# Soft-routed mixture of experts on one Trainium2 core: two mixed stages become an unmixed P1 pair with a split and an unmixed P2 pair, and the preparation of later weights moves between stages

## The chip, the cores and the metric

The kernel runs on one core of one Trainium2 chip. The metric is the time of one execution in microseconds (us), as the device reports it; lower is better. Times are told as the median of several executions.

## What is computed

```python
probs = softmax(router_logits)                 # [16, 512, 8]
output = zeros((16, 512, 2048))
for e in range(8):
    output += probs[:, :, e:e+1] * matmul(x, expert_weights[e])   # [8192,512] x [512,2048]
```

That is one long matrix product: 8192 tokens by a contraction of 8 x 512 = 4096, in which the left operand is x times a token's probability for the expert, by 2048 columns.

## The kernel before

**Three levels of Strassen-Winograd.** The tokens are cut into 16 pairs q of two blocks of 256 (h = 2q and 2q+1), the experts into two halves of four, the columns into two halves of 1024. A pair needs seven products P1 to P7 in place of eight block products (`product(r, q)`, r from 1 to 7). Each product is 256 tokens by a contraction of 2048 by 1024 columns and is cut once more: `STEPS` = 1, 5, 6, 2, 7, 3, 4, seven steps of 8 matmuls each (128 tokens, 128 of the contraction, 512 columns; `Product.step`). Some steps accumulate on a bank that a Vector addition has just written (`Product.post`).

**Stages.** Two products make a stage (`add`), and TensorE runs their steps in turn: 14 slots of 8 matmuls. Stages 0 to 5 hold P1 of the pairs 2 to 13; stage 6 holds P2 of 13 and P1 of 14, stage 7 P2 of 14 and P1 of 15 (the mixed stages); stages 8 to 14 hold the other P2. From stage 15 on come P5, P6, P7, P4, P3.

**The split.** Where both products of a stage have the same right operand, `third(stage, r)` cuts their steps 1 and 5 a third time: the 4 x 8 matmuls of 512 columns become 14 parts of 4 matmuls of 256 columns (`Third.part`, run by `run_third`), with four more sums `s` of left operands, two partial copies per step on ScalarE and two additions `ps<-ps,d` per step on VectorE. Before the change the stages 0 to 5 are split for P1, 8 to 12 for P2, and six stages of P3. In a split stage the order on TensorE is: the parts x1, x5, q1, q5; slot 12 of the stage before, which was held back; x2, q2, x6, q6; slot 13 of the stage before, also held; x7, q7, x3, q3, x4, q4; then the slots from 4 on.

**Where operands come from.** VectorE multiplies x by probabilities into tiles `z` (`times`), and makes sums `s`, `s2` (tile `d`) and `i` (`z<-z,d`, `queue_i`). These are tasks of one queue, written out by a planner (`slack`, `need`, `later`) that keeps two clocks and fixes the order of VectorE's instructions when the program is built; on the chip each engine works strictly in its program's order. Additions of results (`h<-ps,h`) and `ps<-ps,d` are not in the queue: they stand in the program at their step.

**x blocks.** A block of x that is not yet kept transposed is read with a cast by GpSimd's queue (`XBlock.begin`, at the stage two ahead, slot 1) and turned by four transposing DMAs of SyncE's queue for two blocks (`XBlock.finish`, slot 7, line 463). The raw block goes into a buffer of `xpool` (9 buffers), or, for h in `X_ROOMS`, into half of a tile `u`, which two blocks share (`x_room`). There is one buffer of `u`.

**Wedges and casts.** A wedge (`wedge`, `wedge_at`) makes an eighth of the weights for P5, P6 and P7: it casts two blocks of expert weights into a tile `w` by GpSimd's queue, and some slots later (`then`) queues three tasks on VectorE: t3, which writes a tile `u` (the same single buffer), t1 and t2; each is followed by a store to DRAM (`wd<-u`, `wd<-w`) on GpSimd's queue. `cast21` casts the blocks of B21, the raw weights of P2, by the same queue; `sums_at` then queues their sums.

**Results.** P1's results go to DRAM (`kept<-h`), and P2 adds them: it fetches them again on SyncE's queue (`fetch_at`, `h<-kept`) or, where P1 of the same pair has just run, takes the tile (`base = products[1, q].o`).

**Queues.** SyncE (lines 123 and 463), GpSimd (line 126) and ScalarE issue DMAs in order: one that has to wait for its buffer holds everything behind it on that queue.

Of the kernel before, what the change touches and what calls it, by code (L numbers as in the profile page):

```python
# [31 lines left out]
def kernel(  # L32
# [78 lines left out]
    def tt(o, a, b, op):  # L111
        dve(nc.vector.tensor_tensor(out=o, in0=a, in1=b, op=op))  # L112
# [12 lines left out]
    def pool(o, i, **how):  # L125
        note(nc.gpsimd.dma_start(out=o, in_=i, **how))  # L126
# [15 lines left out]
    def new_z():  # L142
        return zpool.tile([P, K8, HQ], f16, name="z", tag="z")
# [248 lines left out]
    queue = deque()  # L392
    clock = {"pe": 0.0, "dve": 0.0}

    class Task:
# [5 lines left out]
        def run(self):  # L401
            self.done = True
            clock["dve"] += self.cost
            self.make()
# [5 lines left out]
    def need(task):  # L410
        if task is not None and not task.done:
            flush(task)
            clock["pe"] = max(clock["pe"], clock["dve"])

    def later(cost, make, first=False):
        t = Task(cost, make)
        (queue.appendleft if first else queue.append)(t)
        return t

    def slack(slot=SLOT):  # L420
        if clock["pe"] > 30.0:
            clock["dve"] = max(clock["dve"], clock["pe"])
        clock["pe"] += slot
        while queue and clock["dve"] < clock["pe"] - LAG:
            queue.popleft().run()
# [3 lines left out]


    x_dram = {}
    X_ROOMS = range(16, 28, 2)
    rooms = {}

    def x_room(h):

        if h % 4 == 0:
            two = new_u().rearrange("p (two k) t -> p two (k t)", two=2)
            for i in range(2):
                rooms[h + 2 * i] = two[:, i].rearrange("p (j m) -> p j m", j=HQ // P)  # L440
        return rooms.pop(h)

    class XBlock:
# [5 lines left out]
        def begin(self):  # L449
# [5 lines left out]
            elif self.t is None:  # L455
                self.xs = x_room(self.h) if self.h in X_ROOMS else xpool.tile([P, HQ // P, H], f16, name="xs", tag="x")
                pool(self.xs, x_f[ds(self.h * HQ, HQ), :].rearrange("(j p) h -> p j h", p=P))
# [34 lines left out]
    class Left:  # L492
# [48 lines left out]
                tt(self.s2, self.t[0][:, :, ds(HP, HP)], self.t[0][:, :, ds(0, HP)], SUB)  # L541
            self.task["s2"] = later(0.61, make)

        def queue_i(self):
            if self.into is not None:
                self.queue_make(1)

            def make():
                self.i = new_z()
                two = "p k (h t) -> p h k t"  # L550
                tt(self.i.rearrange(two, h=2), self.t[1].rearrange(two, h=2),
                   self.s2.unsqueeze(1).to_broadcast([P, 2, K8, HP]), SUB)
            self.task["i"] = later(1.14, make)

        def op(self, p):
            need(self.task[{1: 0, 5: 0, 6: "s2", 2: 1, 4: 1, 3: "i", 7: "i"}[p]])
# [168 lines left out]
    def out_rows(q, odd, cols, tn):  # L725
        t, n = tn
        return out_f[ds((2 * q + odd) * HQ + t * HP, HP), ds(cols * NH + n * NB, NB)]

    def to_out(q, odd, cols, **how):
        return lambda tn, o: pool(out_rows(q, odd, cols, tn), o, **how)  # L730
# [20 lines left out]
    def at(stage, slot, make):  # L751
        hooks.setdefault((stage, slot), []).append(make)

    def add(*products):
        stages.append(products)
        return len(stages) - 1
# [40 lines left out]
    def kept_rows(q):  # L797
        return lambda tn: kept[q][tn[1], ds(tn[0] * HP, HP), :]

    def product(r, q, **how):  # L800
        left, loads = left_of(r, q)
        lefts[r, q] = left
        p = None
        if r == 1:
            def sink(tn, o):
                pool(kept_rows(q)(tn), o)
            p = Product(right[1], left, sink)
        elif r == 2:
            if q >= 13:
                base = products[1, q].o.__getitem__  # L810
            else:
                base = bases[2, q] = Base(kept_rows(q))
            p = Product(right[2], left, to_out(q, 0, 0), base)
        elif r == 5:
            bases[6, q] = m1 = Base(kept_rows(q))
            m1.task = {}

            p = Product(right[5], left, to_out(q, 1, 0))
        elif r == 6:
            m1 = bases[6, q]  # L820

            def base(tn):
                need(m1.task[tn])
                return m1.t[tn]
            p = Product(right[6], left, to_out(q, 0, 1), base)
            if q in KEEP:
                left.kept = dram.tile([P, 2, K8, HQ], f16, name=f"kept_left_{q}")
        elif r == 7:
            if q < 14:
                base = bases[7, q] = Base(lambda tn: out_rows(q, 0, 1, tn))  # L830
            else:
                base = products[6, q].o.__getitem__
            p = Product(right[7], left, to_out(q, 1, 1), base)
        elif r == 4:
            p = Product(right[4], left, to_out(q, 1, 0, accum_op=ADD), products[7, q].o.__getitem__)
        else:
            p = Product(right[3], left, to_out(q, 0, 1, accum_op=ADD), **how)
        p.loads = loads
        products[r, q] = p
        return p  # L840

    products = {}
    forget = lambda *hs: [xs.pop(h, None) for h in hs]
# [30 lines left out]
    thirds, splits, held = {}, {}, []  # L874
# [20 lines left out]
    def before(stage, n):  # L895
        for make in hooks.get((stage, n), ()):
            make()

    def after(stage, n):
        if n == 1:  # L900
            queue_lefts(stage + 1)
        if n == late.get(stage, 1):
            start_loads(stage + 2)
        if n == 5:
            store_loads(stage + 1)
        if n == 7:
            finish_loads(stage + 2)

    def run_third(stage):
# [15 lines left out]
                product.post(p)  # L925
        after(stage, 4)

    def run(stage):
        some = stages[stage]
        for p in some:  # L930
            p.left.queue_i()
        slots = [(p, i) for i in range(len(some[0].steps)) for p in some]

        def one(n):
            p, i = slots[n]
            before(stage, n)
            p.step(p.steps[i])
            slack()
            p.post(p.steps[i])
            after(stage, n + 1)  # L940
        first = 0
        if stage in thirds:
            run_third(stage)
            first = 4
        end = len(slots) - (2 if stage + 1 in thirds else 0)
        for n in range(first, end):
            one(n)
        for n in range(end, len(slots)):
            held.append(lambda n=n: one(n))
# [3 lines left out]
            at(stage, slot, lambda tn=tn: base.fetch(tn))  # L953


    for q in range(2, 14, 2):
        add(product(1, q), product(1, q + 1))
    for q in range(13, 15):
        add(product(2, q), product(1, q + 1))
    forget(*range(0, 26, 2))  # L960
    rest = [15] + list(range(13))
    for i in range(0, 14, 2):
        k = add(product(2, rest[i]), product(2, rest[i + 1]))
        for slot, tn in zip((8, 10, 12, 13), INNER):
            for q in rest[i:i + 2]:
                if q < 13:
                    fetch_at(k if tn == (1, 0) else k - 1, 3 if tn == (1, 0) else slot, bases[2, q], tn)
    xs.clear()
    k5 = add(product(5, 0), product(5, 1))
# [3 lines left out]
    some = product(6, 15)  # L973
# [5 lines left out]
    some = product(4, order7[-1])  # L979
# [50 lines left out]
            send("t2", b)  # L1030
        return casts, [t3, t1, t2]

    def wedge_at(stage, slot, kn, e, then):
        made = []

        def begin():
            casts, made_ = wedge(kn, e)
            casts[0]()
            made.extend(made_ + casts[1:])

        def go_on():
            for make in made[:3]:
                later(1.14, make)
        at(stage, slot, begin)
        at(stage, slot + 4, lambda: made[3]())
        at(*then, go_on)

    b21, t1, t2, t3 = {}, {}, {}, {}

    def cast21(kn, e):  # L1050
        if e == 0:
            b21[kn] = new_w()
        cast_w(21, kn, e, b21[kn][:, ds(e * C, C), :])

    for i, kn in enumerate(((0, 0), (0, 1), (1, 1), (1, 0))):
        for e in range(2):
            at(*((i + 0,5), (i + 0,12))[e], lambda kn=kn, e=e: cast21(kn, e))

    def sums_at(stage, slot, r, of, ps):
        def go():  # L1060
            if right[r].w is None:
                right[r].sums = right[r].build(of)
            for p in ps:
                right[r].queue_sum(right[r].sums, p)
        at(stage, slot, go)
    sums_at(5, 4, 2, b21, (5,))
    sums_at(5, 6, 2, b21, (6,))
    sums_at(5, 8, 2, b21, (7,))
    sums_at(5, 12, 2, b21, (4,))
    for i, (kn, e) in enumerate((kn, e) for kn in ((0, 0), (1, 0), (1, 1)) for e in range(2)):  # L1070
        wedge_at(4 + i, 3, kn, e, {5:(10,6)}.get(i,(4+i,11)))

    def fetch_at_w(stage, slot, of, what, kn):
        at(stage, slot, lambda: of.__setitem__(kn, fetch_w(what, kn)))
# [4 lines left out]
    made = {}  # L1079
# [193 lines left out]
            post(p)  # L1273
    finish.step, finish.post = step_at_end, post_at_end

    for stage in (0,1,2,3,4,5):
        third(stage, 1)
    splits[1].t = early_t
    for stage in (8,9,10,11,12):
        third(stage, 2)  # L1280
    at(7,2, splits[2].queue)

    for q in KEEP:
        for k, slot in enumerate((1, 5)):
# [61 lines left out]
```

## Time and profile before

| | us |
|---|---|
| median of 3 runs (lowest to highest) | 1365.53 (1364.66 to 1365.61) |
| the profiled execution | 1364.02 |
| its span, from the first to the last instruction | 1362.1 |
| TensorE busy | 1355.7 (100%) |
| VectorE busy | 1149.8 (84%) |
| GpSimd busy (it issues DMAs) | 409.4 (30%) |
| ScalarE busy | 203.6 (15%) |

The profile names engines PE (TensorE's matmuls), PEld (its weight loads), DVE (VectorE), ACT (ScalarE), POOL (GpSimd) and SP (SyncE; SPq and POOLq are their queues). A row of the timeline gives the start and the length in us, the engine, the line, the operation with the tiles it writes and reads (out<-in), and how often it stands in a row; in brackets stands the idle time ahead of it and what ended it. A row of the waits gives who waited for whom: us in total, how often, the longest. In rows of the windows, the busy time of each engine in a stretch is followed by its count of instructions. Matmuls overlap, so the length of one is not the pace: the pace is read from starts.

### The profile page before, as it was taken

To read this page: it belongs to the slowest core of one execution; us is meant where nothing else is said; L and a number is where in the kernel's file an instruction comes from. 1 tells how busy PE (TensorE), PEld (TensorE's weight loads), DVE (VectorE), ACT (ScalarE), POOL (GpSimd) and SP (SyncE) were. 2 spreads that over 40 slices of the span, in tenths; PEclk is the share of its full clock that TensorE was granted. 3 is DMA by queue.
4 is the path that set the end of the run, shared out by engine and by line. 5 is a ranking of instruction groups with operands and counts; after the bars stand their busy time and mean duration, and the time that the engine had idled before them with its cause. 6 is when DMAs were issued, how large, how long until landed. Compare 5 with 4: busy or idle time off the path is not lost.

```text
span 1362.1 us, 18545 instructions
## 1 busy us (share of the span) xinstructions
PE 1355.7 (100%) x6801; PEld 662.8 (49%) x6801; DVE 1149.8 (84%) x1415; ACT 203.6 (15%) x386; POOL 409.4 (30%) x644
## 2 busy tenths in 40 slices
PE   9999999999999999999999999999999999999998
PEld 4555545565444444444444444444444444456554
DVE  7976789988999788787887888888889797998873
ACT  3332311111011111111111100000000000123221
POOL 3123233322223333324332122332333322232232
PEclk9999999999999999999999999999999999999999
DMA  9999999999999999999999977988898979999897
GB/s 192 229 249 247 232 232 310 286 309 356 314 307 273 315 339 286 294 280 281 328 275 334 351 241 206 221 246 204 230 243 234 241 204 296 291 223 247 198 206 117
DMA packets 195691, 356.43 MB, mean 262 GB/s; under 512 B 53136, under 2 KB 87184, under 8 KB 191248
## 3 DMA queue, kind: packets, MB, share of 16 engines
q0 software_dynamic: 88048, 183.02, 56.7%
q1 hardware_dynamic: 99488, 132.25, 32.3%
q10 hardware_dynamic: 8064, 39.99, 8.0%
q8 instruction: 53, 0.87, 0.3%
q14 instruction: 38, 0.31, 0.1%
HBM read 214.47 MB, written 167.97 MB: 281 GB/s over the span
## 4 chain that ended last, share of the span: by engine, by line
PE 98%; DMA 1%; issue 1%; POOL 0%; DVE 0%; ACT 0%; POOLq 0%
PE ps L132 98%; DMA w<-in_expert_weights_dram 1%; DMA out_dram<-h 0%; POOL w L126 0%; POOL kept L126 0%; POOL out_dram L126 0%; DVE h L112 0%; ACT h L638 0%; ACT h L1270 0%; DVE ps L112 0%; POOL ident L216 0%; POOLq L126 0%; POOLq L216 0%; POOLq L1330 0%
## 5 line engine op out<-in xcount | busy, mean ns | idle before, releaser
L132 PE MATMUL ps<-w,z 128*128 128x512 f16 x5144 | 1098.4, 373 | 0.4 <-DMA w<-in_expert_weights_dram 0.3
L132 PEld LDWEIGHTS <-z 128*128 128x128 f16 x5280 | 516.4, 98 | 578.1 <-DMA w<-in_expert_weights_dram 0.5
L126 POOL DMA_DIRECT2D out_dram<-h x380 | 249.4, 662 | 739.5 <-ACT h L638 366.1
L112 DVE TENSOR_TENSOR h<-ps,h 128x512 f32<-128x512 f32 x415 | 284.3, 687 | 157.5 <-PE ps L132 137.2
L112 DVE TENSOR_TENSOR z<-xT,pT 128x2048 f16<-128x2048 f16 x216 | 261.7, 1218 | 2.9 <-DMA xT<-w 2.9
L132 PE MATMUL ps<-w,d 128*128 128x512 f16 x880 | 199.1, 379 | 0.0
L132 PEld LDWEIGHTS <-d 128*128 128x128 f16 x880 | 86.1, 98 | 100.3
L112 DVE TENSOR_TENSOR z<-z,d 128x2048 f16<-128x2048 f16 x110 | 131.6, 1217 | 0.0
L638 ACT COPY h<-ps 128x512 f32<-128x512 f32 x64 | 37.6, 587 | 492.5 <-PE ps L132 486.8
L112 DVE TENSOR_TENSOR w<-w 128x1024 f16<-128x1024 f16 (+2 forms) x88 | 100.1, 1146 | 0.8
L627 ACT COPY h<-ps 128x512 f32<-128x512 f32 x90 | 52.8, 587 | 282.8 <-PE ps L132 267.2
L112 DVE TENSOR_TENSOR d<-z 128x1024 f16<-128x1024 f16 x110 | 74.4, 687 | 1.4
L624 ACT COPY h<-ps 128x512 f32<-128x512 f32 x90 | 51.7, 590 | 126.7 <-PE ps L132 119.8
L126 POOL DMA_DIRECT2D kept<-h x56 | 30.6, 547 | 106.7 <-ACT h L627 72.7
L132 PEld LDWEIGHTS <-s 128*128 128x128 f16 x544 | 53.2, 98 | 10.8 <-issue 1.3
L126 POOL DMA_DIRECT2D wd<-w x78 | 46.5, 621 | 38.4 <-DVE w L112 32.6
L132 PE MATMUL ps<-t,s 128*128 128x256 f16 x408 | 55.7, 273 | 0.8 <-DVE ps L112 0.8
L126 POOL DMA_DIRECT2D w<-in_expert_weights_dram x65 | 48.8, 771 | 11.9 <-issue 8.0
L112 DVE TENSOR_TENSOR ps<-ps,d 128x256 f32<-128x256 f32 x68 | 28.4, 430 | 24.9 <-PE ps L132 24.8
L112 DVE TENSOR_TENSOR ps<-ps,h 128x512 f32<-128x512 f32 (+1 forms) x66 | 45.1, 687 | 4.4 <-PE ps L132 4.1
L112 DVE TENSOR_TENSOR u<-xT,pT 128x2048 f16<-128x2048 f16 x38 | 46.3, 1217 | 0.0
L112 DVE TENSOR_TENSOR h<-h 128x512 f32<-128x512 f32 (+2 forms) x69 | 45.2, 675 | 0.1
(63 smaller groups left out, 365.2 us busy)
## 6 DMA issues: line engine op xcount, KB each, us to landing
out_dram<-h POOLq DMA_DIRECT2D x380, 256.0 KB, 6.9
pT<-p_dram SPq DMA_DIRECT2D x125, 256.0 KB, 6.8
h<-kept SPq DMA_DIRECT2D x116, 256.0 KB, 7.9
w<-wd ACTq DMA_DIRECT2D x25, 1024.0 KB, 11.0
xT<-x SPq DMA_DIRECT2D x76, 256.0 KB, 6.5
w<-in_expert_weights_dram POOLq DMA_DIRECT2D x35, 512.0 KB, 10.4
wd<-w POOLq DMA_DIRECT2D x64, 256.0 KB, 6.3
h<-out_dram SPq DMA_DIRECT2D x60, 256.0 KB, 5.6
```

Source lines behind the costliest of these rows:

```text
L112: dve(nc.vector.tensor_tensor(out=o, in0=a, in1=b, op=op))
L126: note(nc.gpsimd.dma_start(out=o, in_=i, **how))
L132: note(nc.tensor.matmul(ps, z, w, start=start, stop=stop, skip_group_check=True))
L624: act(nc.scalar.copy(o[tn], q if p == 5 else x))
L627: act(nc.scalar.copy(o[TN[p]], b if p == 2 else x))
L638: act(nc.scalar.copy(o[tn], b))
```

## The change

Stages 6 and 7 become P1 of the pairs 14 and 15, which is split too, and P2 of 14 and 15; P2's other pairs follow in stages 8 to 14 as 0 to 13, of which 13 now fetches its P1 result from DRAM. The task `i` of a stage goes into VectorE's queue right behind that stage's other tasks in place of the end, for stages 1 to 14. The six wedges begin in stages 1, 2, 3, 6, 7, 8 in place of 4 to 9; the eight casts of B21 move from stages 0 to 3 to stages 3 to 6; P2's sums move by a stage, and the queueing of P2's split weights from stage 7, slot 2 to stage 6, slot 13. `X_ROOMS` becomes h = 24, 26, 28, 30 in place of 16 to 26.

```diff
-    X_ROOMS = range(16, 28, 2)
+    X_ROOMS = range(24,32,2)
...
-        def queue_i(self):
+        def queue_i(self, place=None):
             if self.into is not None:
                 self.queue_make(1)
+            if place is None or self.into is not None:
+                place = len(queue)
...
-            self.task["i"] = later(1.14, make)
+            self.task["i"] = t = Task(1.14, make)
+            queue.insert(place, t)
...
-            if q >= 13:
+            if q >= 14:
                 base = products[1, q].o.__getitem__
...
+    FIRST = lambda stage: 1 <= stage < 15
...
-        for p in some:
-            p.left.queue_i()
+        mine = [t for p in some for t in p.left.task.values()]
+        place = max((i + 1 for i, t in enumerate(queue) if t in mine), default=0) if FIRST(stage) else None
+        for i, p in enumerate(some):
+            p.left.queue_i(None if place is None else place + i)
...
-    for q in range(2, 14, 2):
+    for q in range(2, 16, 2):
         add(product(1, q), product(1, q + 1))
-    for q in range(13, 15):
-        add(product(2, q), product(1, q + 1))
-    forget(*range(0, 26, 2))
-    rest = [15] + list(range(13))
-    for i in range(0, 14, 2):
+    forget(*range(0, 28, 2))
+    rest = [14, 15] + list(range(14))
+    for i in range(0, 16, 2):
...
-                if q < 13:
+                if q < 14:
...
-    def wedge_at(stage, slot, kn, e, then):
+    def wedge_at(stage, slot, kn, e, then, apart=4):
...
-        at(stage, slot + 4, lambda: made[3]())
+        at(stage, slot + apart, lambda: made[3]())
...
+    CASTS = ((3,8),(3,11),(4,4),(4,9),(5,0),(5,5),(5,10),(6,2))
...
-            at(*((i + 0,5), (i + 0,12))[e], lambda kn=kn, e=e: cast21(kn, e))
+            at(*CASTS[2 * i + e], lambda kn=kn, e=e: cast21(kn, e))
...
-    sums_at(5, 4, 2, b21, (5,))
-    sums_at(5, 6, 2, b21, (6,))
-    sums_at(5, 8, 2, b21, (7,))
-    sums_at(5, 12, 2, b21, (4,))
+    sums_at(6, 4, 2, b21, (5,))
+    sums_at(6, 6, 2, b21, (6,))
+    sums_at(6, 8, 2, b21, (7,))
+    sums_at(6, 12, 2, b21, (4,))
+    WEDGES = ((1,3,(1,11),4),(2,3,(2,11),4),(3,2,(3,9),4),(6,2,(6,11),4),(7,8,(8,7),4),(8,9,(9,9),4))
...
-        wedge_at(4 + i, 3, kn, e, {5:(10,6)}.get(i,(4+i,11)))
+        wedge_at(*WEDGES[i][:2], kn, e, *WEDGES[i][2:])
...
-    for stage in (0,1,2,3,4,5):
+    for stage in range(7):
         third(stage, 1)
...
-    at(7,2, splits[2].queue)
+    at(6,13, splits[2].queue)
```

## The prediction, made before the changed kernel had run

> **What bounds the kernel now.** I read the head of the page and its chain first, then the waits of TensorE, then the windows of one stage each, and last the timelines of the queues where the change puts work.
>
> ```profile
> span 1362.1 us, 18545 instructions
> ...
> PE 98%; DMA 1%; issue 1%; POOL 0%; DVE 0%; ACT 0%; POOLq 0%
> ```
> ```profile
> PE ps L132 <- DVE ps L112: 0.8, 1, 0.8
> PE ps L132 <- DMA w<-in_expert_weights_dram: 0.3, 1, 0.3
> PE ps L132 <- DVE h L112: 0.3, 1, 0.3
> ```
>
> The chain is TensorE from end to end, and after its first instruction it stands idle for 1.4 us behind other engines in the whole run. So the time is TensorE's count of columns at its pace plus what stalls a change removes or adds. A gain can come only from fewer columns (little) or from those two DVE waits (1.1 us). A loss has no such bound: whatever makes VectorE late makes TensorE late.
>
> ```profile
> 107.50:130.90 23.40, 23.40 (x138) 13.35 (x137) 15.17 (x20) 6.95 (x14) 7.38 (x13) 1.00 1.16 225
> 177.60:201.80 24.20, 24.20 (x114) 10.95 (x113) 19.93 (x21) 4.09 (x7) 8.66 (x15) 1.00 0.96 218
> 226.20:250.60 24.40, 23.64 (x137) 13.28 (x136) 23.59 (x34) 3.05 (x7) 9.38 (x16) 1.00 1.00 294
> ```
>
> These are stages 3, 6 and 8 (length, then busy PE, PEld, DVE, ACT, POOL, the granted clock, DMA's share). VectorE is busy for 15.2 us of 23.4 in stage 3, but for 23.6 of 24.4 in stage 8, where the longer of TensorE's two DVE waits lies (PE is busy for 23.64 there). The change takes wedges and the split weights out of stages 7 and 8 and puts wedges into stages 1 to 3. In busy time that is right: a wedge's three tasks fit into stage 3's 8 us of idle time. The DMA column says that transfers overlap everywhere; a stage with room on VectorE has none there.
>
> **The change part by part.** The split of the new P1 pair. TensorE's pace comes from starts in stage 3:
>
> ```profile
> 115.29 1.04 PE L132 MATMUL ps<-w,s 128*128 128x256 f16 x8
> 116.17 1.04 PE L132 MATMUL ps<-t,z 128*128 128x256 f16 x8
> 117.04 3.62 PE L132 MATMUL ps<-w,d 128*128 128x512 f16 x16
> 120.49 10.96 PE L132 MATMUL ps<-w,z 128*128 128x512 f16 x52
> ```
> ```profile
> 136.07 1.89 PE L132 MATMUL ps<-w,z 128*128 128x512 f16 x8
> 137.80 0.38 PE L132 MATMUL ps<-t,s 128*128 128x256 f16 x2
> ```
>
> Sixteen matmuls of 256 columns take 117.04 - 115.29 = 1.75 us, 16 of 512 take 120.49 - 117.04 = 3.45 us. Unsplit, steps 1 and 5 of two products are 32 x 0.2156 = 6.90 us; split, 56 x 0.1094 = 6.13. **-0.8 us.** (The two last rows are slot 13 of stage 3 and part x7 of stage 4.) The four sums and four additions that the split adds on VectorE, and its copies on ScalarE, lie under stage 6 (DVE 19.93 of 24.20, ACT 4.09): nothing. P2 of pair 13 fetches four tiles more on SyncE, a stage ahead of their use: nothing; uncovered, one such transfer would cost some 8 us, by the nearest rows below.
>
> The waits of stages 7 and 8. The split weights are queued 3 slots earlier (3 x 1.73 = 5 us), and no wedge's tasks fall between stage 6, slot 11 and stage 8, slot 7. I let both waits go: **-1.1 us**; next late there is nothing that the waits show. The place of `i` changes only the order within VectorE's queue; in stages with idle time that costs nothing, in full ones (stages 11 and 12) I allow 0.5 us either way.
>
> B21's casts and sums, the later wedges: the same work, 5 to 15 us ahead of its use; nothing.
>
> **The wedges in stages 1 to 3 and the one buffer of u.** This is the term that decides. Three kinds of work use that buffer in turn: t3 of wedge 2 writes it (VectorE), its store reads it (GpSimd's queue), two x blocks for stage 5 are cast into it (GpSimd's queue, stage 3, slot 1), four transposes read it (SyncE's queue), and then t3 of wedge 3 (stage 3, slot 9) may write it. Before, wedges begin when the last x block has left u, so the ring was never closed. VectorE's order in the changed program puts t3 of wedge 3 between the first and the second result addition of stage 3's last slots, so if t3 waits, everything behind it waits. The program's waits confirm that this t3 waits for all four transposes and for its own casts. I follow the ring with rows of before at the same places:
>
> ```profile
> 87.99 1.45 POOL L126 DMA_DIRECT2D u<-in_x_dram  x2 [1.79 <-DMA xT<-u]
> ```
> ```profile
> 99.92 0.54 POOL L126 DMA_DIRECT2D kept<-h  x1 [6.41 <-ACT h L627]
> ```
> ```profile
> 109.36 1.45 POOL L126 DMA_DIRECT2D u<-in_x_dram  x2
> ```
> ```profile
> L126 POOL DMA_DIRECT2D w<-in_expert_weights_dram x6: 758/778/785, 64.2 to 116.1; - x6
> ...
> DMA to landing us min/median/max: 8.6/10.6/12.0
> ```
> ```profile
> L126 POOL DMA_DIRECT2D wd<-w x10: 715/720/735, 158.1 to 264.2; - x10
> L126 POOL DMA_DIRECT2D wd<-u x6: 537/540/542, 156.3 to 304.7; - x6
> ...
> DMA to landing us min/median/max: 2.9/5.9/10.8
> ```
> ```profile
> 94.24 5.94 SPq L463 DMA_TRANSPOSE xT<-u  x4
> ```
> ```profile
> 115.23 7.71 SPq L463 DMA_TRANSPOSE xT<-u  x4
> ```
> ```profile
> L463 SPq DMA_TRANSPOSE xT<-u x8: 1288/1438/2797, 94.2 to 120.2; - x8
> ...
> DMA to landing us min/median/max: 5.9/7.8/11.7
> ```
> ```profile
> xT<-u SPq DMA_TRANSPOSE x8, 8.2
> ```
> ```profile
> 154.74 1.22 DVE L112 TENSOR_TENSOR u<-w 128x2048 f16<-128x2048 f16 x1 [1.29 <-DMA w<-in_expert_weights_dram]
> 155.89 0.68 DVE L112 TENSOR_TENSOR h<-ps,h 128x512 f32<-128x512 f32 x1
> 156.49 2.48 DVE L112 TENSOR_TENSOR w<-w 128x2048 f16<-128x2048 f16 x2
> ```
>
> The first bracket shows the ring in small: GpSimd already waits 1.79 us for transposes to free u. Now the steps. Wedge 2's second cast stands behind the store at 99.92, so it is issued at 100.5 and lands 10.6 us later (the median of the casts' view): 111.1. t3 takes 1.2, the store follows 0.3 later (155.96 to 156.3 in before): 112.6. It lands 5.9 later: 118.5. Only then can GpSimd issue the two x casts, which before went out at 109.36. From the first cast to the fourth transpose's landing: the transposes begin 6.25 later (94.24 - 87.99) or 5.87, their issue lasts 5.94 or 7.71, and the last lands 8.2 - 1.4 = 6.8 after the end of its issue: 19.0 or 20.4. I take 19.0, since GpSimd's queue has had a pause: **u is free at 137.5.** A second lock says nearly the same: wedge 3's second cast stands behind both x casts, three stores of 0.54 to 0.72, the first cast (0.78) and one store more, so it is issued at 123.3 and lands at 133.9.
>
> What waits for t3 (the rows of VectorE above, and these):
>
> ```profile
> 131.72 2.35 DVE L112 TENSOR_TENSOR z<-z,d 128x2048 f16<-128x2048 f16 x2
> 135.91 0.87 DVE L112 TENSOR_TENSOR ps<-ps,d 128x256 f32<-128x256 f32 x2 [1.83 <-PE ps L132]
> ```
>
> In the rows above VectorE stands once behind a t3 whose cast is late, for 1.29 us. The order behind t3 is now h, t1, h, t2, h, two i, ps: by starts 1.15 + 0.6 + 1.14 + 0.6 + 1.14 + 0.6 + 2.3 + 0.45 = 8.0 us until the addition `ps<-ps,d` that part x7 of stage 4 needs. Undisturbed, x7 starts at 137.80, so t3 may start as late as 129.8 without harm; VectorE itself would reach it at about 127. At 137.5 x7 starts at 145.5: **+7.7 us.** (Slot 13, at 136.07, waits for the first h behind t3, some 3 us; that lies within the 7.7.) Nothing gives it back: TensorE has no slack later.
>
> Bounds of this term: with the longest rows (12.0, 10.8, 20.4) u is free at 145.2, +15.4. With the shortest (8.6, 2.9, and 5.9 for the cast and each transpose: 16.3 in all) at 129.8, just no wait. The medians lie between, and since each of four transfers in a row would have to be short at once, I stay with them.
>
> **The sum.** -0.8 - 1.1 + 7.7 = +5.8 us. The profiled execution took 1364.0 (span 1362.1 and 1.9 around it), so 1369.8 on that scale; the median of the runs shown is 1365.5, 1.5 above the profiled one, and the forecast goes on that scale: **1371.3**.
>
> **Rivals.** (1) *The ring closes in time.* Condition: t3 of wedge 3 starts by 129.8. For it: in the ring only one transfer is under way at a time on GpSimd's queue, and transfers are shorter then; against it, SyncE's and the stores' traffic goes on (DMA share 1.16 in that stage). Then the change is what it looks like by busy time: 1365.5 - 1.9 = 1363.6, not slower. By the Trainium skill, page "DMA: Bandwidth & Descriptors", section "Anatomy of one DMA — SWDGE (gpsimd) path", a transfer takes 2.0 us plus its bytes at 436 GB/s: an estimate of 3.2 us for the store of 512 KB (128 x 2048 f16), and by it this rival would come true; the store's rows here have a median of 5.9. Chance 0.10.
> (2) *A short wait.* The store lands in 2.9 and the rest stays: u is free at 132.5 to 134.5, the wait 2.7 to 4.7, the time 1366.3 to 1368.3. Chance 0.22.
> (3) *The wait also lets TensorE's clock fall.* Between slot 13 and x7 TensorE would idle 8.0 - 1.75 - 1.73 = 4.5 us.
>
> ```profile
> 1.29 4.45 PE L94 MATMUL every<-zero 128*128 128x512 f16 x10 [1.29 <-DVE zero L91]
> 5.80 1.01 PE L132 MATMUL ps<-h,w 128*128 128x128 f16 x8
> ```
>
> At the start of the run ten matmuls of 512 columns take 5.80 - 1.29 = 4.5 us, twice the later pace; a fall of that kind would cost 10 x (0.45 - 0.216) = 2.3 us more: 1373.6. No row of before has such an idle time in mid-run. The Trainium skill, page "TensorE: Matmul & The Clock Gate", section "What's actually happening", says that an idle window of about 3.4 us halves the clock and that the windows run free, so that 4.5 us may or may not hold one. Chance 0.13.
> (4) *The forecast*, a wait of 4.8 to 12 us: 0.52. The rest, 0.03, is for a gain that I don't see.
>
> The blocks h = 16 to 22 now take buffers of the pool of nine, where SyncE's second pair of transposes may wait for the first to land (8.2 us more). VectorE's products for stages 3 and 4 come some 5 us before their use, so I price this at 0 to 2 us, in the range alone.
>
> **Range and chances.** 1365.0 to 1377.0 leaves out rival 1 and the far end of the wait. What a measurement of this kernel can tell from no change is about 0.2%, 2.7 us: slower by more (over 1368.3) is 0.52 + 0.13 and part of rival 2, 0.68; within it 0.29; faster 0.03.
>
> **What would show it.** In the profile after: a wait of VectorE of 8 to 12 us ahead of the third `u<-w`, put down to `xT<-u` or to a cast; GpSimd idle about 6 us for `wd<-u` ahead of `u<-in_x_dram`; TensorE's waits for DVE h and DVE ps near 136 to 146 us, some 7 us in all; none near 219 and 234; 24 matmuls more. If u<-w starts by 130 us, the ring is not what I take it for; if TensorE waits elsewhere, the bound of VectorE's order was misread.

## The result, and the profile after

The changed kernel takes 1375.59 us (median of 4 runs, 1373.94 to 1376.31), the kernel before beside it 1365.1 (4 runs, 1364.37 to 1365.61): a ratio of 1.0072, 95% interval 1.0059 to 1.0086. It is slower by 10.5 us; the forecast was 5.8 slower, so 4.3 us of the measured time were missing from it; the range of 1365.0 to 1377.0 held, near its upper end. The profiled execution took 1375.44.

The page of the changed kernel, its head and its chain:

```profile
span 1373.6 us, 18625 instructions
...
PE 96%; DVE 1%; DMA 1%; issue 0%; SPq 0%; POOL 0%; ACT 0%; DVEq 0%; POOLq 0%
```

TensorE's share of the chain has fallen from 98% to 96%. That is not the loss itself, since the chain also runs through VectorE where TensorE is busy. TensorE's longest waits (us in total, times, longest):

```profile
PE ps L132 <- DVE h L112: 6.3, 2, 6.0
PE ps L132 <- DVE ps L112: 3.7, 2, 2.5
...
```

The chain in order of time tells where (its pieces up to the loss, shorter ones left out: start, length, what):

```profile
10.04 111.90 PE ps L132 x653
123.15 2.27 DVE z L112 x2
126.18 2.18 SPq L463
128.40 11.35 DMA xT<-u
141.62 1.22 DVE w L112
143.35 1.21 DVE w L112
145.16 2.27 DVE z L112 x2
147.82 170.59 PE ps L132 x960
```

Read it backwards from 147.82: TensorE waited for VectorE, which had the wedge's sums (`w`) and `i` (`z`) to do, and VectorE had waited for a transposing DMA of SyncE's queue into `xT` out of `u`, 11.35 us from issue to landing. TensorE's timeline of that place:

```profile
134.74 1.04 PE L132 MATMUL ps<-t,s 128*128 128x256 f16 x8
141.75 3.57 PE L132 MATMUL ps<-w,z 128*128 128x512 f16 x8 [5.97 <-DVE h L112]
147.82 1.87 PE L132 MATMUL ps<-t,s 128*128 128x256 f16 x8 [2.50 <-DVE ps L112]
149.49 1.86 PE L132 MATMUL ps<-w,s 128*128 128x256 f16 x8
151.19 1.04 PE L132 MATMUL ps<-t,z 128*128 128x256 f16 x8
```

Beside the two waits there is a second thing: slot 13 (at 141.75) takes 3.57 us for 8 matmuls that took 1.89 before, and from 147.82 to 151.19 each 8 matmuls of 256 columns take 1.7 us from start to start, where 0.87 was the pace. The windows of those 20 us agree (the third number from the end is the granted clock):

```profile
130.00:140.00 10.00, 5.78 (x43) 4.08 (x42) 0.13 (x1) 1.88 (x5) 0.00 (x0) 1.00 1.18 238
140.00:150.00 10.00, 5.75 (x19) 2.65 (x19) 9.84 (x13) 0.59 (x1) 7.72 (x12) 0.55 0.90 258
```

VectorE is busy for 0.13 us of the first ten: it stands. In the ten behind them the granted clock is 0.55.

Where the time went, by the start of each stage on TensorE, after less before (both profiled executions):

| place | us |
|---|---|
| up to stage 0 | -0.46 |
| stage 4: x7 10.48 late, and the half pace behind it 1.61 | +12.09 |
| the split of stage 6 | -0.79 |
| the waits of stages 7 and 8, gone | -0.26 and -1.03 |
| stage 11 | +0.37 |
| stage 16 | +1.40 |
| sum | +11.32 |

From stage 17 on the two run alike. The loss at stage 16 has its own rows, one of TensorE and one of VectorE:

```profile
434.91 1.89 PE L132 MATMUL ps<-w,d 128*128 128x512 f16 x8 [1.24 <-DVE ps L112]
```
```profile
406.08 2.29 DVE L112 TENSOR_TENSOR w<-w 128x4096 f16<-128x4096 f16 x1 [0.57 <-DMA w<-wd]
```

The three loads `w<-wd` of ScalarE's queue for the next sums went out 8.3 us after stage 14 began (4.75 before), and the second one, for which VectorE waited here, landed 15.1 us after its issue (14.3 before). By TensorE's shift at that time (9.92 us) VectorE's sums were 0.5 us late ahead of this row, 1.1 with it, and 1.4 at 416.95, where a second wait of 0.20 us, for a cast of weights, was added. So the load makes up a part of the 1.40; where the first 0.5 us come from is not shown.

### The profile page after: what moved, and what is told of

Same layout as the page of the kernel before. It is cut to its first block, busy times and chain, and to the rows that moved or that the text cites. A ratio compares the mean times of both kernels' runs of the same rounds, so it can differ in the third digit from the quotient of the medians.

```text
span 1373.6 us, 18625 instructions
## 1 busy us (share of the span) xinstructions
PE 1357.6 (99%) x6825; PEld 665.5 (48%) x6825; DVE 1153.0 (84%) x1423; ACT 204.6 (15%) x390; POOL 409.6 (30%) x644
## 4 chain that ended last, share of the span: by engine, by line
PE 96%; DVE 1%; DMA 1%; issue 0%; SPq 0%; POOL 0%; ACT 0%; DVEq 0%; POOLq 0%
PE ps L132 96%; DMA xT<-u 1%; DVE z L112 1%; DMA w<-in_expert_weights_dram 1%; DVE h L112 0%; DVE w L112 0%; SPq L463 0%; DVE d L112 0%; POOL w L126 0%; DVE ps L112 0%; ACT h L1277 0%; DVEq L112 0%; POOL ident L216 0%; POOLq L216 0%; DVE u L112 0%
## 5 line engine op out<-in xcount | busy, mean ns | idle before, releaser
L627 ACT COPY h<-ps 128x512 f32<-128x512 f32 x90 | 51.6, 590 | 117.1 <-PE ps L132 114.2
L132 PEld LDWEIGHTS <-s 128*128 128x128 f16 x576 | 57.1, 99 | 14.2 <-issue 3.5
L132 PE MATMUL ps<-t,s 128*128 128x256 f16 x432 | 59.8, 275 | 2.5 <-DVE ps L112 2.5
```

Source lines behind the costliest of these rows:

```text
L132: note(nc.tensor.matmul(ps, z, w, start=start, stop=stop, skip_group_check=True))
L627: act(nc.scalar.copy(o[tn], q if p == 5 else x))
```

## The experiments

**Theory A:** the loss at stage 4 is the one buffer of `u`, which closes a ring: t3 of wedge 2, its store, two x casts, four transposes, then t3 of wedge 3; and VectorE's strict order passes the wait on. **Rival B:** wedge 3's late second cast alone would do nearly as much. **Rival C:** a lack of buffers or of room on the DMA engines. **Rival D:** the other parts of the change cost something. All ratios are against the kernel before, with 95% intervals; the chips of the experiments had it at 1365 to 1366.

**Two buffers of u.**

```diff
-        return zpool.tile([P, K8, HQ], f16, name="u", tag="u", bufs=1)
+        return zpool.tile([P, K8, HQ], f16, name="u", tag="u", bufs=2)
...
-    hpool = ctx.enter_context(tc.tile_pool(name="hpool", bufs=13))
+    hpool = ctx.enter_context(tc.tile_pool(name="hpool", bufs=11))
```

> The changed kernel with two buffers of u instead of one (h tiles 11 instead of 13, which pays for its 4 KB of each partition). Theory A (the single buffer of u closes a ring: wedge 2's t3 and store hold it until 113.9 us, only then do x's casts for stage 5 start, and wedge 3's t3 waits for their transposes until 139.9): x's casts start at stage 3's first slot, 5 us or more earlier, the transposes have landed near 131 to 133, wedge 3's t3 follows within 2 us of that or of its own second cast, and the wait of 5.97 us ahead of slot 13 shrinks below 2 us: 1363.5 to 1367. Theory B (wedge 3's second cast, issued at 118.9 and landed at 133.6, is the lock that counts): t3 stays near 134 to 136 and 3 to 6 us remain: 1367 to 1371. Theory C (eleven h tiles are too few, or the DMA engines are simply full then): no better than 1374.

Measured: 1371.02, ratio 1.0045 (1.0028 to 1.0061). **The same ring opened from the other side**, by giving the blocks back to the x pool:

```diff
-    X_ROOMS = range(24,32,2)
+    X_ROOMS = range(28,32,2)
```

> The changed kernel with the blocks h = 24 and 26 in rooms of the x pool again, not in u (h = 28 and 30 stay in u): the three wedges, the late casts of B21, the new pair and i's place as in the changed kernel. A: the ring between u's store and the x casts is open, so the casts do not wait for wedge 2's store; t3 of wedge 3 waits only for its own casts: wait ahead of slot 13 below 2 us, 1363.5 to 1367. B (the second cast of wedge 3): 1367 to 1371. C (the x pool of nine is too small for these two as well, and the wait moves to the loads of stages 5 and 6): a wait of TensorE on z<-xT,pT at stage 5 or 6, 1368 or more.

Measured: 1368.5, ratio 1.0021 (1.0009 to 1.0032). VectorE's timeline, first with two buffers, then with the x pool, and TensorE's of the latter:

```profile
133.19 1.22 DVE L112 TENSOR_TENSOR u<-w 128x2048 f16<-128x2048 f16 x1 [6.99 <-DMA w<-in_expert_weights_dram]
```
```profile
132.75 1.23 DVE L112 TENSOR_TENSOR u<-w 128x2048 f16<-128x2048 f16 x1 [6.36 <-DMA w<-in_expert_weights_dram]
```
```profile
140.70 1.86 PE L132 MATMUL ps<-t,s 128*128 128x256 f16 x8 [2.97 <-DVE ps L112]
142.36 1.91 PE L132 MATMUL ps<-w,s 128*128 128x256 f16 x8
```

In both, t3 of wedge 3 comes 7 us earlier than in the changed kernel (139.87), and the releaser is another: the cast, no longer the transposes. So A is true for the part from 133 to 140 and B for the part from 130 to 133: two locks behind one another. Opening the first leaves a wait of 3.0 to 3.6 us with half pace after it. With two buffers 2.04 us more were lost at stage 12 (a wait of 1.87 us for `z`), which the eleven h tiles may have cost; that was not separated. With the x pool no wait for `z<-xT,pT` appeared at stage 5 or 6, so the part of C about a lack of buffers did not show there.

**t3 of wedge 3 later.**

```diff
-(3,2,(3,9),4)
+(3,2,(4,6),4)
```

> The changed kernel with one edit: wedge 3's three subtractions are queued at stage 4, slot 6 (about 141 us) instead of stage 3, slot 9 (about 122 us). The ring stays as it is, the transposes still land near 139.8 us, but VectorE passes stage 4's work first. Theory A and B alike: the wait of VectorE is below 2 us, none of the 5.97 and 2.50 us of TensorE is left, and with them goes the half pace up to 151 us: 12.1 us less, 1363.5. If VectorE then stalls at the same t3 somewhat later, with stage 4's last evacuations behind it, 1365 to 1370. If the transposes come later still and stage 5's first operand is late: 1368 or more.

Measured: 1370.41, ratio 1.0039 (1.0027 to 1.0052): a miss, close to the second case, in which VectorE stalls at the same t3 later. VectorE's and TensorE's timelines:

```profile
158.19 1.23 DVE L112 TENSOR_TENSOR u<-w 128x2048 f16<-128x2048 f16 x1 [8.70 <-DMA xT<-u]
```
```profile
161.32 5.28 PE L132 MATMUL ps<-w,z 128*128 128x512 f16 x16 [5.79 <-DVE h L112]
```

The wait at stage 4 is gone and stands at stage 5 with the same releaser. Queued at slot 6, t3 comes behind the x blocks h = 28 and 30 (begun at slot 1), which take the same buffer: it waits for their transposes, a turn of the ring later. This is the clearest sign of the ring, and it says that a place has to be found behind both pairs of blocks.

**The regrouping alone**, and **the regrouping with i ahead**. The first diff is of both, the second of the first one only; P2's sums and its split weights stay where the change puts them:

```diff
-    X_ROOMS = range(24,32,2)
+    X_ROOMS = range(16,28,2)
...
-    CASTS = ((3,8),(3,11),(4,4),(4,9),(5,0),(5,5),(5,10),(6,2))
+    CASTS = ((0,5),(0,12),(1,5),(1,12),(2,5),(2,12),(3,5),(3,12))
...
-    WEDGES = ((1,3,(1,11),4),(2,3,(2,11),4),(3,2,(3,9),4),(6,2,(6,11),4),(7,8,(8,7),4),(8,9,(9,9),4))
+    WEDGES = ((4,3,(4,11),4),(5,3,(5,11),4),(6,3,(6,11),4),(7,3,(7,11),4),(8,3,(8,11),4),(9,3,(10,6),4))
```
```diff
-        place = max((i + 1 for i, t in enumerate(queue) if t in mine), default=0) if FIRST(stage) else None
+        place = None
```

> The new pair alone: a seventh split P1 stage and an eighth P2 stage instead of the two mixed ones, with the kernel before's casts of B21, six wedges, rooms of u (h = 16 to 26) and i at the queue's end; only the four sums of B21 are queued one stage later, since P2 begins one stage later. Theory A (all of the loss comes from the moved wedges and rooms): the split's 0.8 and the two waits' 1.3 us are gained and nothing is lost: 2.1 less than before, 1363.0. Theory D (the regrouping itself costs: the 0.37 and 1.40 us that the changed kernel lost at stages 12 and 16): 1364.8. If the sixth wedge or a room collides with the new pair, over 1366.

> The regrouping with the kernel before's casts, wedges and rooms, as in the earlier run of the regrouping alone, but with i ahead of other sums. There TensorE waited for i (z<-z,d) at 219.5, 245.2, 272.6 and 322.0 us, 0.42 + 2.12 + 2.12 + 0.86 us, each behind the three sums of a wedge, and lost 8.5 us from stage 6 to 12 with the half pace that followed. If i's place decides: these waits go, 0.5 us at 185 stays, and the end is the kernel before less the split's 0.8 and the 1.1 us of its waits: 1363 to 1364.5. If i only changes places with the wedge, and the wedge's sums or the next operands (z<-xT,pT, the transposes of u's rooms) are late instead: 1366 to 1371.

Measured: 1371.94, ratio 1.0044 (1.0031 to 1.0056), and 1374.73, ratio 1.0068 (1.0052 to 1.0084). So the pair without the moved wedges loses as well, though not at stage 4: D in its strong form, and a miss for the expectation that nothing else costs. VectorE's and TensorE's timelines of the first, and TensorE's of the second:

```profile
240.26 1.21 DVE L112 TENSOR_TENSOR u<-w 128x2048 f16<-128x2048 f16 x1
241.51 2.48 DVE L112 TENSOR_TENSOR w<-w 128x2048 f16<-128x2048 f16 x2
243.91 2.35 DVE L112 TENSOR_TENSOR z<-z,d 128x2048 f16<-128x2048 f16 x2
```
```profile
245.19 9.20 PE L132 MATMUL ps<-w,z 128*128 128x512 f16 x36 [2.12 <-DVE z L112]
```
```profile
278.03 0.61 PE L132 MATMUL ps<-t,s 128*128 128x256 f16 x4 [1.85 <-DVE s L112]
```

VectorE has no idle time from the wedge's three sums (3.65 us by starts) to `i`, and `i` is 2.1 us late. Put `i` ahead and `s` of the next stage is late instead (1.06, 1.85 and 1.06 us at 251.9, 278.0 and 326.4): a swap, as the rival said. That is not all of the second one's loss: near stage 16 TensorE waits 2.40 and 2.41 us more, with half pace behind the latter. I read this as a need of the new pair to have wedges out of these stages, and the stages to which the change moves them are where the changed kernel pays; no run has the new pair without any wedges there.

**The clock.** 37 matmuls that add zero, in the idle stretches around slot 13 (`none` is a tile of zeros; 22 behind slot 12, 15 behind slot 13, in stage 4 alone; the lines that set these counts are left out here):

```diff
             for k in range(K8):
                 mm(self.banks[b], z[:, k, :], w[:, k, :], p in (1, 5) and k == 0, k == K8 - 1)
+            for _ in range(busy.pop()):
+                mm(self.banks[b], none, w[:, 0, :], False, False)
+            busy.append(0)
```

> The changed kernel plus 37 matmuls that add zero, in the two idle stretches around slot 13 of stage 3: 22 of 512 columns behind slot 12 and 15 behind slot 13, into banks that are open anyway, so that nothing of VectorE's work is added or moved and the same t3 ends the waits at the same times. They take 4.8 and 3.2 us at full pace and so leave under 1.5 us idle in one piece. If the half pace after 141.75 us comes from the idle (the clock falls): slot 13 takes 1.73 instead of 3.57 us, the parts from 147.8 run at full pace, and the end comes 1.6 us earlier: span 1372.0 for 1373.6. If the half pace has another cause (the transposes and casts that load the memory at that time): slot 13 and the parts stay at 430 and 215 ns a matmul and the added matmuls run late, 1373.6 or more.

Measured: 1372.46, ratio 1.0056 (1.0043 to 1.0069), span 1370.6. TensorE's timeline, and the window to set beside the one above:

```profile
134.07 4.91 PE L132 MATMUL ps<-w,none 128*128 128x512 f16 x22
...
141.70 1.89 PE L132 MATMUL ps<-w,z 128*128 128x512 f16 x8 [0.97 <-DVE h L112]
143.42 3.40 PE L132 MATMUL ps<-w,none 128*128 128x512 f16 x15
147.77 1.03 PE L132 MATMUL ps<-t,s 128*128 128x256 f16 x8 [0.95 <-DVE ps L112]
148.64 1.04 PE L132 MATMUL ps<-w,s 128*128 128x256 f16 x8
```
```profile
140.00:150.00 10.00, 8.08 (x50) 4.66 (x49) 10.00 (x14) 1.16 (x2) 7.73 (x12) 1.00 0.91 255
```

VectorE's waits end at the same times and x7 starts at 147.77 for 147.82; slot 13 is back at 1.72 us (141.70 to 143.42) and the clock at 1.00. TensorE reaches the part after x7, q7, x3 and q3 at 150.44 for 152.06: the lower clock behind the idle time cost 1.6 us. Most of the rest of the 3.0 us by which the span is shorter is stage 16, which lost 0.17 us here and 1.40 there.

**i's place**, in the changed kernel (undone, as in the regrouping alone) and in the kernel before (done: `queue_i` and `run` as in the change).

> The changed kernel with i at the queue's end, as in the kernel before. If the i order matters where a wedge's or other sums stand in the queue ahead of it, TensorE waits for z<-z,d at stages 7 to 9, where the last three wedges are (two waits of about 2.1 us with half pace after them, 3 us each): 1378 to 1382. If i's place is worth nothing here, as I forecast (within 0.5 us): 1375 to 1376, and the 0.37 us at stage 12 goes with it.

> The kernel before with one part of the change alone: i ahead of other sums in stages 1 to 14. I forecast no more than 0.5 us for i's place; in the changed kernel the undoing of it cost 2.7 us, where wedges' sums stand ahead of i. Here wedges 1 to 6 and the sums of B21 share the queue with i in stages 4 to 10: if the gain of i's place is general, its 0.8 us of waits at stages 7 and 8 go, 1364 to 1364.8; if it is only a swap (what was ahead of i, s and z of the next stage, is late in its place, as in the regrouping with i ahead, 1374.7), 1366 to 1370.

Measured: 1378.28, ratio 1.0095 (1.008 to 1.011), and 1376.55, ratio 1.0067 (1.0044 to 1.009). Undone in the changed kernel, TensorE waits at stage 3. VectorE's timeline, then TensorE's:

```profile
112.85 2.47 DVE L112 TENSOR_TENSOR w<-w 128x2048 f16<-128x2048 f16 x2
115.24 0.76 DVE L112 TENSOR_TENSOR ps<-ps,d 128x256 f32<-128x256 f32 x2
```
```profile
115.72 1.03 PE L132 MATMUL ps<-t,s 128*128 128x256 f16 x8 [1.78 <-DVE ps L112]
```

There t1 and t2 of wedge 2 (`w`) stand ahead of the addition `ps<-ps,d` that x7 needs; in the kernels with i ahead the addition comes first. The 1.99 us lost at stage 3 are the largest piece of the difference in the profiled executions. In the medians of four runs each, 2.7 us, the two intervals still touch. The waits that I expected at stages 7 to 9 did not come; one of 0.87 us came at stage 10. Done in the kernel before, it costs 11 us of median (6 runs, 1368.03 to 1379.75), by waits that neither expectation named. VectorE's and TensorE's rows:

```profile
193.69 2.29 DVE L112 TENSOR_TENSOR w<-w 128x4096 f16<-128x4096 f16 x1 [4.25 <-DMA wd<-w]
```
```profile
197.78 2.53 PE L132 MATMUL ps<-w,z 128*128 128x512 f16 x11 [3.42 <-DVE h L112]
```

A sum of weights waits there until a store has freed its tile, and stage 16 loses 5.26 us more. So the order of `i` has no worth of its own: the same step cost time in one kernel and, by the profiles, saved some in the other, and what differs between them is which wedges and sums share the queue.

**Mending it.** With the blocks in the x pool as above, wedge 3's second cast one slot after the first:

```diff
-(3,2,(3,9),4)
+(3,2,(3,9),1)
```

> The changed kernel with h = 24 and 26 in the x pool (the earlier run that left 2.97 us of wait) and one more edit: wedge 3's second cast one slot after its first instead of four. Theory: two locks lie behind one another, the ring of u (t3 at 139.9 us) and behind it wedge 3's second cast (landed 132.7 us in that run, t3 at 132.8). With the cast issued near 116 instead of 119.1 us it lands near 129.5, t3 starts by 130, and none of the 2.97 us nor the half pace after it is left: 5 to 6 us less than that run's 1368.5, 1362.8 to 1364. Rival: the casts share full DMA engines, and the second lands near 132 however early it is issued: 1366.5 to 1368.5.

Measured: 1367.14 over 12 runs from 1363.2 to 1370.47, ratio 1.0011 (1.0001 to 1.0022): a miss in the median; the profiled run is the fastest, span 1361.1. VectorE's timeline in it:

```profile
129.64 1.23 DVE L112 TENSOR_TENSOR u<-w 128x2048 f16<-128x2048 f16 x1 [3.54 <-DMA w<-in_expert_weights_dram]
```

129.64 is just inside the bound (129.8 by the forecast's count), and TensorE waits 0.16 us. The cast went out 2.6 us earlier than with the x pool alone and landed 3 us earlier, so full DMA engines (the other part of C) did not hold it back in this execution. Both locks open, the loss is gone, but where the cast lands a few us later it comes back; that is how I read the spread, since only one run has a trace. The next one moves the wedge instead, with `X_ROOMS` as in the change:

```diff
-(3,2,(3,9),4)
+(4,11,(5,9),2)
```

> The changed kernel with one wedge moved: wedge 3's casts at stage 4, slots 11 and 13 (was stage 3, slots 2 and 6) and its sums at stage 5, slot 9 (was stage 3, slot 9). Its t3 is then queued near 170 us, behind both pairs of x blocks that use u, whose transposes landed by 158 us in the run with the late t3, and its casts, issued near 150 and 153, should land by 167. Theory A with both locks (ring and second cast), each out of VectorE's way by 3 us or more: no wait at stage 4 nor at stage 5, no half pace, 12.1 us less than the changed kernel, 1361.5 to 1363.5, and with less scatter from run to run than the kernel with the early cast, whose t3 came at 129.64 us against a bound of 129.8. Rivals: the sums find VectorE full at stage 5 and push i or stage 6's operands (a wait of 1 to 2 us with half pace there): 1364 to 1367; or the second loss at stage 16 (1.4 us in the changed kernel) is still there: 1363 to 1365.

Measured: **1363.57** over 12 runs (1361.54 to 1372.88), ratio 0.9986 (0.9968 to 1.0004): 12.0 us less than the changed kernel, and 1.85 less than the kernel before in the median, which the interval does not quite tell from no change. One run of 1372.88 says that the smaller scatter which I expected is not shown. Stage 4 and stage 5 have no wait, and stage 16 has none either, as in the runs with the x pool and the late t3; its 1.40 us came and went with the other edits. What is left stands at stage 3, in VectorE's and TensorE's timelines:

```profile
111.18 1.23 DVE L112 TENSOR_TENSOR u<-w 128x2048 f16<-128x2048 f16 x1 [4.74 <-DMA w<-in_expert_weights_dram]
```
```profile
115.67 1.03 PE L132 MATMUL ps<-t,s 128*128 128x256 f16 x8 [1.34 <-DVE ps L112]
```

The last two start from this kernel: wedge 2's second cast two slots earlier, and with that `i` at the queue's end from stage 11 on (the second diff, of the last one only).

```diff
-(2,3,(2,11),4)
+(2,3,(2,11),2)
```
```diff
-    FIRST = lambda stage: 1 <= stage < 15
+    FIRST = lambda stage: 1 <= stage < 11
```

> The kernel with wedge 3 moved to stages 4 and 5, and one more edit: wedge 2's second cast two slots after its first instead of four. In that kernel's profile VectorE waited 4.74 us for this cast (issued 100.23, landed 111.05 us), x7 of stage 3 came 1.34 us late, and 1.55 us were lost. Issued near 96.8 it lands near 107.5, t3 starts with it and x7 is on time: 1.5 us less than 1363.6, 1361.5 to 1362.5, and faster than the kernel before beyond the interval. Rival: the earlier cast only lengthens the stores of wedge 1 ahead of it (11.7 us) and lands at the same time: 1363 to 1364.5.

> The same kernel with i ahead of other sums only in stages 1 to 10 instead of 1 to 14, so that in stages 11 and 12 it stands at the queue's end again as in the kernel before. Every kernel with i ahead lost 0.37 us at stage 11 to 12, where TensorE waited 0.19 us for z<-xT,pT; those with i at the end lost 0.86 us near 303 or 322 us where a wedge's sums or the next operand came first. If i's swap with stage 12's operand is the cause of the 0.37: 0.3 to 0.4 us less than the kernel with both wedges moved. If the end of the queue costs more there: 0.5 us more.

Measured: 1367.6 (12 runs, 1362.5 to 1374.36), ratio 1.0011 (0.9992 to 1.003), and 1369.16 (12 runs, 1361.98 to 1370.9), ratio 1.0011 (0.9996 to 1.0026): misses. In the first one's profile the 1.55 us at stage 3 are gone as expected, but 6.3 us are lost at stage 6. Its VectorE and its TensorE, and then the same 10 us of the DMA engines, in this kernel and in the one with wedge 3 alone moved (DMA share and GB/s are the last two numbers):

```profile
181.15 1.23 DVE L112 TENSOR_TENSOR u<-w 128x2048 f16<-128x2048 f16 x1 [5.51 <-DMA w<-in_expert_weights_dram]
```
```profile
189.11 1.87 PE L132 MATMUL ps<-t,s 128*128 128x256 f16 x8 [4.19 <-DVE ps L112]
```
```profile
155.00:165.00 10.00, 10.00 (x72) 6.86 (x71) 5.20 (x7) 4.60 (x10) 2.61 (x4) 1.00 1.33 132
```
```profile
155.00:165.00 10.00, 10.00 (x76) 7.17 (x74) 6.84 (x9) 3.18 (x8) 5.21 (x8) 1.00 1.13 293
```

Wedge 3's second cast lands at 181.1 in place of 172.4; it was issued 1.7 us later and took 18.8 us in place of 11.8, while the DMA engines were busier and moved less than half the bytes. The four transposes before it took 9.9 to 16.0 us from issue to landing in the one and 4.6 to 6.7 in the other. The ring of `u` is still in both: the x casts ahead of these transposes had to wait for it, 8.38 us in the one and 3.73 in the other. Whether the edit does that, or whether it comes and goes by itself (the runs of the first one are 1362.5 to 1364 in five cases of 12, 1366 or more in the others), stays open, and with it whether this kernel has fewer losses than the one with wedge 3 alone moved. Nor does the 0.37 us at stage 11 follow from i's place in the queue there: it is in the second one as well (0.37).

## Why the prediction was right, step by step

*The split, -0.8:* right, -0.79. *The waits of stages 7 and 8, -1.1:* right, -0.26 - 1.03 = -1.29.

*The ring, +7.7:* right in every link and short in size: x7 came 10.48 late. GpSimd's queue and SyncE's queue in the changed kernel, then VectorE's t3:

```profile
110.73 0.54 POOL L126 DMA_DIRECT2D wd<-u  x1 [3.65 <-DVE u L112]
...
114.18 1.45 POOL L126 DMA_DIRECT2D u<-in_x_dram  x2 [2.31 <-DMA wd<-u]
```
```profile
122.07 9.83 SPq L463 DMA_TRANSPOSE xT<-u  x4
```
```profile
139.87 1.22 DVE L112 TENSOR_TENSOR u<-w 128x2048 f16<-128x2048 f16 x1 [13.71 <-DMA xT<-u]
```

The sub-steps were mis-sized in opposite ways. Wedge 2's second cast landed at 109.1 and not at 111.1, and the store landed 3.2 us after its issue, not 5.9, so the x casts went out at 114.2 and not at 118.5. By the Trainium skill, page "DMA: Bandwidth & Descriptors", section "Anatomy of one DMA — SWDGE (gpsimd) path", 3.2 us was the estimate for this store, and here the trace agrees; but this kernel's six stores of that size took 2.9 to 8.9 us, and the 256 KB casts behind this one took 7.9 and 8.8 us, for which the same rule gives an estimate of 2.6. Nor does the short store alone let the ring close in time, as the prediction has it under rival 1: by its own sum 112.6 + 3.2 + 19.0 = 134.8 is past 129.8.

Then the step "I take 19.0, since GpSimd's queue has had a pause" failed: from the first x cast to the last transpose's landing it took 25.6 us (114.18 to 139.75), longer than either total worked out from before, 19.0 or 20.4. What the wait had held back (two x casts, two weight casts, two stores `wd<-w`, results) went out in one burst from 114.2 to 119.7, ahead of the transposes, whose issue alone lasted 9.83 us (5.94 and 7.71 in the rows of before). It is tempting to blame the pause and the burst, but the runs do not bear that out: with two buffers of `u`, where the x casts did not wait for the store, the same stretch took 28.5 us; with wedge 3's weight casts moved out of the burst it took 21.8, and in the two kernels made from that one 27.4 and 31.0. What the length goes with is the number of other transfers under way when the first transpose was issued: 3 to 5 where it took 18.5 to 21.8 us (two rows of before, and wedge 3 moved), 8 in the changed kernel, 7 to 10 in the six experiments with 25.7 to 31.0. That the crowding is the cause fits all ten, and no run tests it alone. So the two errors, 4.3 us early and 6.6 us late, cancelled in part, and that t3 came only 2.4 us behind the forecast is in part luck.

From t3 to x7 the working held: 7.95 us for 8.0. The second lock was forecast to issue at 123.3 and land at 133.9; it issued at 118.9 and landed at 133.6, and the runs with the ring open showed it to be a lock of its own, worth 3 to 3.6 us of wait.

*Rival 3, the clock:* it came true together with the forecast's wait, and more widely than I had it: I looked for the idle time between slot 13 and x7, but the 6 us ahead of slot 13 had already lowered the clock. Its price was 1.6 us, by the run that filled the idle time, in place of 2.3. Together 7.7 + 2.3 would have been 10.0, against 12.1 measured for the stage.

*The signs:* TensorE's waits came where they were forecast, 8.5 us for some 7, and there are 24 matmuls more. VectorE's wait ahead of t3 was 13.7 us for 8 to 12, GpSimd's for the store 2.3 us for 6.

*The order of i, within 0.5 us:* wrong as a statement on the change, as far as the profiles show. Without it the changed kernel waited at stages 3 and 10 as well, 2.7 us in the medians. I had looked at its cost where VectorE is full, and not at what the early wedges put into the queue behind it.

*Not foreseen:* stage 16, +1.40, and stage 11, +0.37. For the first I had followed VectorE's and GpSimd's queues and not ScalarE's loads some 240 us behind the ring; what holds those loads back is not shown. The 0 to 2 us for the x pool cost TensorE nothing: SyncE's second pair of transposes did wait for the first to land, from 98.2 to 107.0 us, but TensorE has no wait there.

## What to carry to other kernels

Count the users of a single buffer in the order in which the program asks for it; if one of them stands in an engine that must not wait, place it behind all the others' last readers, and look for the second lock behind the first. Work moved into idle time of an engine also moves its transfers, which meet others there; price those by rows that had as many other transfers under way, and with wide bounds. And a place that holds by 0.2 us in one trace is not a safe place: the kernel with wedge 3 a stage and a half later has a median 3.6 us below the one with the cast 2.6 us earlier, though both profiled spans are within 1.0 us of each other.

## What the runs showed of the hardware

TensorE's clock falls after shorter idle times than I had reckoned with, and not always; the length of one idle time does not decide it. The regrouping with `i` ahead has two of the same length in one run:

```profile
424.81 7.07 PE L132 MATMUL ps<-w,z 128*128 128x512 f16 x32 [2.40 <-DVE h L112]
434.28 3.54 PE L132 MATMUL ps<-w,d 128*128 128x512 f16 x8 [2.41 <-DVE ps L112]
```

Behind the first, 32 matmuls run at full pace; behind the second, 8 take 3.37 us from start to start where 1.73 is the pace. In the regrouping alone 2.12 us were enough (at 245.19; 36 matmuls took 9.04 us from start to start where 7.76 is the pace), and in the kernel before with `i` ahead 3.42 us at 197.78 were not (80 matmuls in 17.26 us, full pace). The traces' records of the granted clock explain the difference. In the middle of a run it is 1.00 or 0.50, and the stretches at 0.50 last 3.41, 6.83 or 10.24 us: one, two or three steps of 3.41. I laid a grid of that step through each of the 14 traces, from its own clock edges, and added up TensorE's idle time in each step. At full clock, behind the 12 steps with 2.03 us idle or more the clock was halved; behind every step with 1.95 or less it was not. The 2.40 us above fell into two steps (1.59 and 0.81), the 2.41 nearly whole into one (2.36), and the 3.42 into two (1.95 and 1.47). A halved clock came back behind a step with at most 0.36 us idle, and stayed behind those with 0.82 or more. By the Trainium skill, page "TensorE: Matmul & The Clock Gate", section "What's actually happening", the clock halves after an idle window of about 3.4 us, and the windows run free: the traces agree with the length and the free run, but a window does not have to be idle from end to end, since 2.03 us of 3.41 were enough here.

How long a transfer takes goes with what is under way when it is issued, and not with a pause of its queue. The same store of 512 KB (`wd<-u`) stands six times in each of the 14 traces, 84 times in all. With at most four other transfers of the core under way at its issue it took 2.9 to 8.4 us, median 3.5 (29 stores); with seven or more, 5.2 to 15.0, median 7.3 (29 stores). Behind a pause of GpSimd of more than 2 us it took 2.9 to 10.1. This is how they go together, not an experiment on it.

The DMA engines can be busier and move less: 132 GB/s at a share of 1.33 beside 293 at 1.13 in the two windows above. In the first the transposes out of `u` were still under way, and 983 of 1667 packets were under 512 B; in the second they had landed at 154.5, and 144 of 1878 were.
